# Down projection of a gated MLP in seven half-size products: where two operand sums are formed, who orders VectorE, how far ahead loads are issued, and how the last bank is stored

## The chip, the cores and the metric

The kernel runs on one core of one Trainium2 chip, in one launch that computes one decoder layer. The metric is the device time of the launch in microseconds (us): before the change 1162.03 us, the median of three runs (1159.37, 1162.03 and 1162.38 us).

## What is computed

The layer has three mixing branches (attention, convolution, pooling), an output projection, and a gated MLP. Only the MLP's last step, and the end of the step before it, are touched by the change:

```python
h2 = rms_norm(x, norm2_g[l])
up = h2 @ w_up[l].astype(h2.dtype)                 # 1024 x 5632
up = causal_depthwise_conv(up, ffn_dw_w[l])        # three taps
gate, val = jnp.split(up, 2, axis=-1)
x = x + (jax.nn.silu(gate) * val) @ w_down[l].astype(up.dtype)   # (1024 x 2816) @ (2816 x 1024)
```

All tensors are float32. Call A = silu(gate) * val (1024 tokens x 2816 features), B = w_down, C = A B.

## The kernel before

**Three matmuls for one product.** The matmuls take operands of type fp32r, and each float32 operand is split into two of them: ScalarE casts the high part (`dh`, line 48), VectorE subtracts it from the operand to get the low part (`dl`, line 49). `mm3` (lines 51 to 55) then issues three matmuls, high x high (line 53), high x low (54) and low x high (55). `split` is one such pair of a cast and a subtraction.

**The up projection** runs over 22 feature tiles f, `up(f)` (line 773). Its tail for each f: the last products `prod(..., "3")` and `"22"`; VectorE adds their banks into the tile `u` (line 803 for the value half `uv`, 805 for the gate half `ug`); the three taps are done by ScalarE (768) and twice by VectorE (770); the product `"4"` reuses the bank `b1` that line 803 has read; ScalarE copies it out (812); GpSimd multiplies gate and value (814) and writes the tile to DRAM as `gd[f]` (815). The buffers of pool `ep` (4 buffers) hold `u`, `ws`, `wsh`, `wsl` during this stage; pool `wx` (1 buffer) holds the raw weights `wur`.

**The down projection** starts at line 822. A and B are cut into quadrants (tokens or columns into two halves of 512, features into two halves of 11 tiles of 128), and C is formed from seven quadrant products instead of eight, with sums of quadrants as operands. The work runs in four passes over the 11 feature tiles n, with two sets of four PSUM banks, X and Y (one bank for each 128 tokens x 512 columns):

| pass | steps | operands in X | operands in Y | after the pass, VectorE adds |
|---|---|---|---|---|
| a | 11 | A11, B11 | A12, B21 | X and Y to `acc11`, stored |
| b | 11 | S2 = A22+A21-A11, T2 = B22-B12+B11 | S1 = A21+A22, T1 = B12-B11 | X to `acc12`, Y to `acc22` |
| c | 11 | A11-A21, B22-B12 | A12-S2, B22 | X to `acc22`, stored; Y to `acc12`, stored |
| d | 6 (two tiles n a step, the last one) | A22, B21-T2 | none | X to `acc21`, stored |

The banks go on accumulating from pass to pass. A step is 24 matmuls of 128 x 128 by 128 x 512 (12 for each set of banks, and 12 in the last step of pass d): 38 x 24 + 12 = 924 matmuls. `step_mm` (866) writes one set's 12; `prep(p, n)` (902) forms the sums of step (p, n) on VectorE and splits them; `load(p, n)` (883) issues its DMAs on the queue of SyncE (SP) into a buffer `dr`; `ga` and `wb` (828, 832) load a 128 x 512 piece of A (from `gd`) or of B, 256 KB each.

Before the change `prep` of pass b forms all four sums S1, T1, S2, T2, for which A11 and B11 are loaded again; pass c forms A11-A21. Operands kept from pass to pass (`st`, `ab`, `a11`, the trace's `res`) are loaded a few per step by `load_res`. The buffers `dr` go in turn to `wx`, `ep`, `ep` (`raw_home`, 925), and the sums that are loaded from x (`acc12`, `acc22`) lie in two buffers of `ep`.

**What sets the order.** On SP the order is the program's (`manual_schedule`, 928): loads of step i + 2, then kept operands, in each round of the loop. On VectorE, ScalarE and TensorE a scheduler at build time orders the instructions by readiness and priority; the bank additions `add_to` (857) are given high priority. Stores of finished sums (`store`, 862) are DMAs issued by GpSimd (POOL).

## Time and profile before

| what | us |
|---|---|
| median of three runs | 1162.03 |
| the profiled execution, its own time | 1161.21 |
| its span in the trace | 1159.4 |
| VectorE busy, whole span | 882.5 |
| ScalarE busy, whole span | 576.0 |
| GpSimd busy, whole span | 361.4 |

The profile covers one execution. Its page gives busy times by engine, a chain of work followed back from the end, and groups of instructions by line; the trace can be asked for an engine's instructions in order of time, who waited for whom, and what each engine did in a stretch of the span. In a row of the timeline stand the start, the duration, engine, line, operation, written tile <- read tiles, shape, and in brackets the idle time before it and what ended it. The down projection's first matmul starts at 928.6 us and its last at 1151.9 us.

### The profile page before, as it was taken

The numbers are of one execution on the slowest core, as the hardware profiler recorded it, in microseconds if no ns is written. First come the engines' busy times: TensorE is split into PE (matmuls) and PEld (weight loads), VectorE is DVE, ScalarE is ACT, GpSimd is POOL, SyncE is SP. The second block draws the span as 40 slices with busy tenths as digits, with TensorE's granted clock in tenths as the row PEclk, the third lists the DMA queues.
The fourth block names the chain that finished last, engine by engine and source line by source line (L and its number), as shares of the span: only waits on it lengthen the run. The fifth ranks groups of instructions, "written<-read, shape, count | busy, mean of one in ns | idle before, by whom it ended". The sixth has DMA issues, their size and how long they took to land.

```text
span 1159.4 us, 15556 instructions
## 1 busy us (share of the span) xinstructions
PE 1104.9 (95%) x5684; PEld 921.4 (79%) x5684; DVE 882.5 (76%) x1259; ACT 576.0 (50%) x1045; POOL 361.4 (31%) x373
## 2 busy tenths in 40 slices
PE   7999889999999999879999999999999999899996
PEld 6789889978778878758888888888888788688875
DVE  5798974758998756778877888787878755998673
ACT  8322456688998644445443535353535343233331
POOL 1365597867666653101212121212121210000010
PEclk9999999999999999969999999999999999899999
DMA  9220110022111141211222121312221397672372
GB/s 359 72 81 25 40 28 20 15 74 74 55 48 46 47 154 73 109 37 55 89 75 96 68 96 68 105 59 85 79 98 67 117 328 267 240 263 91 128 235 74
DMA packets 51885, 119.99 MB, mean 103 GB/s; under 512 B 6368, under 2 KB 11872, under 8 KB 48992
## 3 DMA queue, kind: packets, MB, share of 16 engines
q1 hardware_dynamic: 46208, 99.06, 25.8%
q0 software_dynamic: 5600, 19.93, 4.3%
q8 instruction: 45, 0.74, 0.3%
q14 instruction: 32, 0.26, 0.1%
HBM read 94.84 MB, written 19.92 MB: 99 GB/s over the span
## 4 chain that ended last, share of the span: by engine, by line
PE 69%; DVE 10%; issue 7%; DMA 5%; ACT 4%; POOL 3%; SPq 1%; POOLq 0%; ACTq 0%; DVEq 0%
PE b L53 12%; PE b L55 12%; PE b L54 12%; PE mm L53 3%; PE mm L55 3%; PE mm L54 3%; DVE dl L49 3%; PE s L499 2%; DVE acc L257 2%; PE t L523 2%; DMA dr<-in_w_down_dram 2%; PE c L53 1%; PE c L55 1%; PE c L54 1%; DMA dr<-gd 1%
## 5 line engine op out<-in xcount | busy, mean ns | idle before, releaser
L814 POOL TENSOR_TENSOR ac<-ac 128x1024 f32<-128x1024 f32 x22 | 61.5, 2793 | 367.9 <-ACT u L795 207.3
L770 DVE SCALAR_TENSOR_TENSOR ac<-u,par,ac 128x1023 f32<-128x1023 f32 x88 | 112.7, 1280 | 9.6 <-ACT ac L768 8.7
L53 PE MATMUL mm<-w,hh 128*128 128x256 f32 (+1 forms) x384 | 110.3, 288 | 8.5 <-DVE qk L445 4.6
L54 PE MATMUL mm<-w,hh 128*128 128x256 f32 (+1 forms) x384 | 109.5, 285 | 0.6 <-POOL w L49 0.6
L55 PE MATMUL mm<-w,hl 128*128 128x256 f32 (+1 forms) x384 | 109.1, 284 | 0.0
L48 ACT CAST wsh<-ws 128x2048 fp32r<-128x2048 f32 x22 | 42.0, 1910 | 123.5 <-PE b L54 123.3
L257 DVE SCALAR_TENSOR_TENSOR acc<-u,par,acc 128x512 f32<-128x512 f32 x120 | 93.3, 835 | 0.0
L49 DVE TENSOR_TENSOR dl<-dr,dh 128x1024 fp32r<-128x1024 f32 (+1 forms) x39 | 65.6, 1684 | 28.0 <-ACT dh L48 24.9
L511 POOL TENSOR_TENSOR p<-p,l 128x896 f32<-128x896 f32 (+3 forms) x64 | 72.6, 1151 | 44.0 <-DVE l L510 37.5
L48 ACT CAST dh<-dr 128x1024 fp32r<-128x1024 f32 (+1 forms) x39 | 54.7, 1401 | 58.4 <-PE y L55 24.7
L53 PEld LDWEIGHTS mm<-w,hh 128*128 128x128 f32 x384 | 73.0, 190 | 10.1 <-DVE fgt L433 4.8
L49 POOL TENSOR_TENSOR w<-wr,w 128x256 fp32r<-128x256 f32 (+1 forms) x56 | 63.9, 1166 | 42.6 <-ACT w L48 42.3
L54 PEld LDWEIGHTS mm<-w,hh 128*128 128x128 f32 x384 | 73.1, 190 | 1.2 <-POOL w L49 0.8
L55 PEld LDWEIGHTS mm<-w,hl 128*128 128x128 f32 x384 | 73.2, 191 | 0.3
L864 POOL DMA_DIRECT2D out_dram<-acc x16 | 8.7, 542 | 206.9 <-DVE acc L860 206.3
L54 PE MATMUL x<-dl,dh 128*128 128x512 f32 x176 | 69.6, 395 | 3.4 <-DVE dl L49 3.4
L55 PE MATMUL x<-dh,dl 128*128 128x512 f32 x176 | 69.3, 394 | 0.0
L768 ACT ACTIVATE ac<-u,par 128x1024 f32<-128x1024 f32 x44 | 50.7, 1152 | 36.3 <-DVE u L805 35.8
L48 ACT CAST dh<-res 128x1024 fp32r<-128x1024 f32 x22 | 23.1, 1051 | 84.2 <-PE y L55 55.7
L49 DVE TENSOR_TENSOR wsl<-ws,wsh 128x2048 fp32r<-128x2048 f32 x22 | 50.4, 2290 | 12.4 <-ACT wsh L48 12.4
L677 DVE TENSOR_TENSOR ws<-wur 128x512 f32<-128x512 f32 x22 | 59.1, 2688 | 0.0
L53 PE MATMUL x<-dh 128*128 128x512 f32 x176 | 54.0, 402 | 5.2 <-DVE acc L860 4.5
(308 smaller groups left out, 3395.1 us busy)
## 6 DMA issues: line engine op xcount, KB each, us to landing
wur<-in_w_up_dram SPq DMA_DIRECT2D x22, 1024.0 KB, 4.9
dr<-in_w_down_dram SPq DMA_DIRECT2D x66, 256.0 KB, 5.1
dr<-gd SPq DMA_DIRECT2D x55, 256.0 KB, 4.3
gd<-ac POOLq DMA_DIRECT2D x22, 512.0 KB, 3.0
res<-gd SPq DMA_DIRECT2D x22, 256.0 KB, 5.6
wr<-in_w_in_dram SPq DMA_DIRECT2D x40, 128.0 KB, 2.1
v<-in_x_dram SPq DMA_DIRECT2D x8, 512.0 KB, 8.4
wor<-in_w_out_dram SPq DMA_DIRECT2D x16, 256.0 KB, 3.0
```

What stands on the lines that cost most here:

```text
L48: nc.scalar.copy(out=dst_hi, in_=src)
L49: (lo or nc.vector).tensor_tensor(out=dst_lo, in0=src, in1=dst_hi.bitcast(F32), op=ALU.subtract)
L53: nc.tensor.matmul(ps, a_hi, b_hi, start=first, stop=False, skip_group_check=more)
L54: nc.tensor.matmul(ps, a_hi, b_lo, start=False, stop=False, skip_group_check=more)
L55: nc.tensor.matmul(ps, a_lo, b_hi, start=False, stop=last, skip_group_check=more)
L257: nc.vector.scalar_tensor_tensor(out=a, in0=u[:, c, o + j:o + j + 512], scalar=pc(PC_DW + c * CW + j), in1=a, op0=ALU.mult, op1=ALU.add)
L499: nc.tensor.matmul(ps[:, 0:c1 - c0], qT[:, i * P:(i + 1) * P], part[:, c0:c1], start=b == 0, stop=b == 1 and c1 < n)
L511: nc.gpsimd.tensor_tensor(out=pt[:, 0:n], in0=pt[:, 0:n], in1=l[:, 1:2].broadcast_to([P, n]), op=ALU.mult)
L677: nc.vector.tensor_tensor(out=out, in0=a, in1=b, op=ALU.subtract)
L768: nc.scalar.activation(out=ac, in_=us, func=AF.Copy, scale=pc(w0 + 2))
L770: nc.vector.scalar_tensor_tensor(out=ac[:, j:S], in0=us[:, 0:S - j], scalar=pc(w0 + 2 - j), in1=ac[:, j:S], op0=ALU.mult, op1=ALU.add)
L814: nc.gpsimd.tensor_tensor(out=a[:, 1], in0=a[:, 1], in1=a[:, 0], op=ALU.mult)
```

## The change

It has five parts.

1. **Two sums move to pass a.** A11-A21 (in `ab`) and T1 (in `st`) are formed in pass a, where A11 and B11 are in the step's buffer anyway; `a11` becomes `a21`, a copy of A21 kept for pass b. Pass b no longer loads B11, and A11 is not loaded a second time. Per n the number of VectorE sums stays 8: before 4 in pass b, 3 in c, 1 in d; now 2 in a, 3 in b, 2 in c, 1 in d. In pass b the split of the second half of the operands becomes two splits of 128 x 512.
2. **VectorE's order is the program's** in the down projection (`manual_schedule` for DVE): each round splits the next step, forms sums of a step two or three rounds ahead, and adds finished banks at written places. In passes a and b the Y banks' matmuls are written ahead of the X banks'. In the last `up`, `issue_after` puts the gate's taps behind the addition of line 803.
3. **Loads are issued four steps ahead** instead of two, all `dr` buffers are the four of `ep`; `acc22` moves to `wx`, `acc12` to pool `mxa`.
4. **The last two steps** of pass d are written bank by bank, each bank's addition right behind it.
5. **The last store** goes out on SP's queue instead of GpSimd's, and that of the last bank in two halves of 256 columns. `acc12` is added and stored in the first step of pass d.

```diff
         prod(b1, sums, 2, "3", False, True)
-        nc.vector.tensor_tensor(out=uv[:, h1], in0=uv[:, h1], in1=b1, op=ALU.add)
+        added = nc.vector.tensor_tensor(out=uv[:, h1], in0=uv[:, h1], in1=b1, op=ALU.add)
...
-        taps3(a[:, 0], ug, 0, f)
+        with tc.issue_after(added.ins) if f + 1 == NF else ExitStack():
+            taps3(a[:, 0], ug, 0, f)
...
-    homes = iter([(s8, "s8")] * 6 + [(hp2, "hx")] * 8 + [(mxa, "mx")] * 2 + [(ep, "ep")] * 2)
+    homes = iter([(s8, "s8")] * 6 + [(hp2, "hx")] * 8 + [(mxa, "mx")])
...
     def add_to(acc, banks):
         for t in range(4):
-            with tc.high_priority():
-                nc.vector.tensor_tensor(out=acc[:, t], in0=acc[:, t], in1=banks[t], op=ALU.add)
+            nc.vector.tensor_tensor(out=acc[:, t], in0=acc[:, t], in1=banks[t], op=ALU.add)
...
     def load(p, n):
-        r = raw_t[p, n] = slot(*raw_home[len(raw_t) % 3], "dr")
+        r = raw_t[p, n] = slot(ep, "ep", "dr")
...
-        elif p == "b":
-            ga(r[:, 0], "22", n)
-            wb(r[:, 1], "11", n)
-            wb(r[:, 2], "22", n)
...
+        elif p in "bc":
+            ga(r[:, 0], "22" if p == "b" else "12", n)
+            wb(r[:, 1], "22", n)
...
+    def sums(p, n):
         r = raw_t[p, n]
-        if p == "b":
-            nc.vector.tensor_tensor(out=r[:, 0], in0=r[:, 0], in1=ab[n][:, 0], op=ALU.add)
-            sub(r[:, 1], ab[n][:, 1], r[:, 1])
-            sub(st[n][:, 0], r[:, 0], a11[n][:, 0])
-            sub(st[n][:, 1], r[:, 2], r[:, 1])
+        if p == "a":
+            sub(ab[n][:, 0], r[:, 0], a21[n][:, 0])
+            sub(st[n][:, 1], ab[n][:, 1], r[:, 1])
+        elif p == "b":
+            sub(st[n][:, 0], r[:, 0], ab[n][:, 0])
+            nc.vector.tensor_tensor(out=r[:, 0], in0=r[:, 0], in1=a21[n][:, 0], op=ALU.add)
...
+        elif p == "b":
+            part(3, 1, st[n][:, 1:2])
+            part(2, 1, r[:, 0:1])
+            sub(st[n][:, 1], r[:, 1], st[n][:, 1])
+            for s_ in between:
+                sums(*s_)
+            yield
+            part(0, 2, st[n])
...
-    AHEAD, ready = 2, None
-    order = ctx.enter_context(tc.manual_schedule(engines={mybir.EngineType.SP}))
+    AHEAD, N = 4, len(steps)
+    sums_in = {i: [steps[i]] for i in range(NH)}
+    for j in range(NH, N):
+        sums_in.setdefault(j - 3 if j < NH + 2 else j - 2, []).append(steps[j])
+    ctx.enter_context(tc.manual_schedule(engines={mybir.EngineType.SP}))
...
+    ctx.enter_context(tc.manual_schedule(engines={mybir.EngineType.DVE}))
+    for i, (p, n) in enumerate(steps):
+        load_res(2)
+        if i + AHEAD < N:
             load(*steps[i + AHEAD])
...
+            h2 = hl_t[steps[i + 1]]
+            for t in (0, 1):
+                bank_mm(X, h, 2, t, False, False)
+                bank_mm(X, h, 0, t, False, False)
+            for t in range(4):
+                if t > 1:
+                    bank_mm(X, h, 2, t, False, False)
+                    bank_mm(X, h, 0, t, False, False)
+                bank_mm(X, h2, 0, t, False, True)
+                for cs in (slice(0, 256), slice(256, 512)) if t == 3 else (halves[0],):
+                    nc.vector.tensor_tensor(out=acc21[:, t, cs], in0=acc21[:, t, cs], in1=X[t][:, cs], op=ALU.add)
+                    nc.sync.dma_start(out=out[(4 + t) * P:(5 + t) * P, cs], in_=acc21[:, t, cs])
```

How the built program's instructions move is seen at three places.

**The first loads, on SP's queue.** These are the eight DMAs of steps (a, 0) and (a, 1), before:

```order
L830 DMA dr<-gd 128x512 [waits DMASW0_49,DMAHW5_49,DVE_49,Activation_49]
L834 DMA dr<-in_w_down_dram 128x512
L830 DMA dr<-gd 128x512 [waits DMASW3_49]
L834 DMA dr<-in_w_down_dram 128x512
L830 DMA dr<-gd 128x512 [waits DVE_49,PE_49,DMASW1_49,Activation_49,Pool_49]
L834 DMA dr<-in_w_down_dram 128x512
L830 DMA dr<-gd 128x512 [waits DMASW4_49]
L834 DMA dr<-in_w_down_dram 128x512
```

and the same eight after:

```order
L831 DMA dr<-gd 128x512 [waits DVE_49,PE_49,DMASW0_49,Activation_49,Pool_49]
L835 DMA dr<-in_w_down_dram 128x512
L831 DMA dr<-gd 128x512 [waits DMASW3_49]
L835 DMA dr<-in_w_down_dram 128x512
L831 DMA dr<-gd 128x512 [waits DMASW1_49,PE_49]
L835 DMA dr<-in_w_down_dram 128x512
L831 DMA dr<-gd 128x512 [waits DMASW4_49]
L835 DMA dr<-in_w_down_dram 128x512
```

The first step's buffer was that of `wx`; now it is the first one that comes free in `ep`, and its first DMA carries the wait for five engines that the second step's first DMA had.

**The last feature tiles and the first steps, on ScalarE and VectorE.** First ScalarE. `u_8337` and `b1_8334` belong to f = 20, `u_8457` to f = 21; `dh_...<-dr_...` 128x2048 are the casts of steps (a, 0) and (a, 1). Before:

```order
L781 COPY u_8457<-b1_8454 128x512
L48 CAST dh_8584<-dr_8574 128x2048
L812 COPY u_8337<-b1_8334 128x512
L810 ACTIVATE ac_8431<-ac_8431 128x1024
L768 ACTIVATE ac_8431<-u_8337,par_68 128x1024
L797 COPY u_8457<-b3_8456 128x512
L795 COPY u_8457<-b1_8454 128x512
L768 ACTIVATE ac_8536<-u_8457,par_68 128x1024
L810 ACTIVATE ac_8536<-ac_8536 128x1024
L48 CAST dh_8609<-dr_8579 128x2048
```

After:

```order
L781 COPY u_8457<-b1_8454 128x512
L813 COPY u_8337<-b1_8334 128x512
L768 ACTIVATE ac_8431<-u_8337,par_68 128x1024
L811 ACTIVATE ac_8431<-ac_8431 128x1024
L797 COPY u_8457<-b3_8456 128x512
L795 COPY u_8457<-b1_8454 128x512
L768 ACTIVATE ac_8536<-u_8457,par_68 128x1024
L48 CAST dh_8614<-dr_8590 128x2048
L813 COPY u_8457<-b1_8454 128x512
L48 CAST dh_8627<-dr_8595 128x2048
```

The first step's cast stood ahead of the copy of f = 20's last bank (line 812, now 813) and of the scaling behind it (768); it now stands behind them and behind all of f = 21 but one copy.

VectorE at the same place: `u_8457` is the last tile `u`; `ac_8536` its taps; `dl_...<-dr_...` the low parts of steps (a, 0), (a, 1) and on. Before:

```order
L49 TENSOR_TENSOR dl_8585<-dr_8574,dh_8584 128x2048
L770 SCALAR_TENSOR_TENSOR ac_8431<-u_8337,par_68,ac_8431 128x1023
L770 SCALAR_TENSOR_TENSOR ac_8431<-u_8337,par_68,ac_8431 128x1022
L805 TENSOR_TENSOR u_8457<-u_8457,b3_8456 128x512
L770 SCALAR_TENSOR_TENSOR ac_8536<-u_8457,par_68,ac_8536 128x1023
L803 TENSOR_TENSOR u_8457<-u_8457,b1_8454 128x512
L770 SCALAR_TENSOR_TENSOR ac_8536<-u_8457,par_68,ac_8536 128x1022
L49 TENSOR_TENSOR dl_8610<-dr_8579,dh_8609 128x2048
```

After:

```order
L770 SCALAR_TENSOR_TENSOR ac_8431<-u_8337,par_68,ac_8431 128x1023
L770 SCALAR_TENSOR_TENSOR ac_8431<-u_8337,par_68,ac_8431 128x1022
L805 TENSOR_TENSOR u_8457<-u_8457,b3_8456 128x512
L803 TENSOR_TENSOR u_8457<-u_8457,b1_8454 128x512
L770 SCALAR_TENSOR_TENSOR ac_8536<-u_8457,par_68,ac_8536 128x1023
L49 TENSOR_TENSOR dl_8615<-dr_8590,dh_8614 128x2048
L770 SCALAR_TENSOR_TENSOR ac_8536<-u_8457,par_68,ac_8536 128x1022
L49 TENSOR_TENSOR dl_8628<-dr_8595,dh_8627 128x2048
```

The addition of line 803 now stands ahead of both taps of the last gate, and the low part of the first step, which stood ahead of all of these, stands behind it.

**VectorE at the change from pass a to pass b.** `x0` to `x3` and `y0` to `y3` are the banks, line 860 (now 856) their addition to `acc11`. Before:

```order
L677 TENSOR_TENSOR res_8595<-res_8600,res_8595 128x512
L905 TENSOR_TENSOR dr_9043<-dr_9043,res_8595 128x512
L860 TENSOR_TENSOR acc_8855<-acc_8855,x1_8565 128x512
L677 TENSOR_TENSOR res_8589<-dr_9003 128x512
L860 TENSOR_TENSOR acc_8855<-acc_8855,x2_8566 128x512
L677 TENSOR_TENSOR dr_9043<-res_8595,dr_9043 128x512
L860 TENSOR_TENSOR acc_8855<-acc_8855,x3_8567 128x512
L860 TENSOR_TENSOR acc_8855<-acc_8855,y0_8568 128x512
L49 TENSOR_TENSOR dl_9014<-res_8588,dh_9013 128x1024
L49 TENSOR_TENSOR dl_9014<-dr_8952,dh_9013 128x1024
```

After:

```order
L677 TENSOR_TENSOR res_8580<-res_8586,dr_8844 128x512
L856 TENSOR_TENSOR acc_8574<-acc_8574,y0_8568 128x512
L856 TENSOR_TENSOR acc_8574<-acc_8574,y1_8569 128x512
L856 TENSOR_TENSOR acc_8574<-acc_8574,y2_8570 128x512
L856 TENSOR_TENSOR acc_8574<-acc_8574,y3_8571 128x512
L49 TENSOR_TENSOR dl_8994<-res_8575,dh_8993 128x1024
L856 TENSOR_TENSOR acc_8574<-acc_8574,x0_8564 128x512
L856 TENSOR_TENSOR acc_8574<-acc_8574,x1_8565 128x512
L856 TENSOR_TENSOR acc_8574<-acc_8574,x2_8566 128x512
L856 TENSOR_TENSOR acc_8574<-acc_8574,x3_8567 128x512
L49 TENSOR_TENSOR dl_9044<-res_8575,dh_9043 128x512
L49 TENSOR_TENSOR dl_9044<-dr_8920,dh_9043 128x512
```

The bank additions, which were mixed with the sums of coming steps, now stand in two runs of four, Y ahead of X, with the split of one operand between them.

On TensorE the last 12 matmuls of the program stand in the same order as before (first the four high x high, then the two others of bank x0, of x1, of x2, of x3). In pass a each step's eight high x high matmuls stand ahead of its sixteen others, Y's banks ahead of X's; at the first step of pass b the order is y0, y1, y2, y3, x0, x1, x2, x3 with all three matmuls of a bank together, and a few high x high matmuls of the step behind it in between.

More of the change, by code (lines that the diff above doesn't have):

```diff
@@ L909, in prep, with halve, part @@
         elif p == "c":
             sub(r[:, 0], r[:, 0], st[n][:, 0])
-            sub(ab[n][:, 0], a11[n][:, 0], ab[n][:, 0])
             sub(ab[n][:, 1], r[:, 1], ab[n][:, 1])
-        elif p == "d":
+        else:
             for j in range(min(2, NH - n)):
                 sub(r[:, 2 * j + 1], r[:, 2 * j + 1], st[n + j][:, 1])
-        h = hilo()
+    def halve(p, n, between=()):
+        r = raw_t[p, n]
+        h = hl_t[p, n] = hilo()
+        def part(i, q, src):
+            split(h[0][:, i:i + q], h[1][:, i:i + q], src)
@@ new lines, in tile_hybrid_block @@
+    AHEAD, N = 4, len(steps)
[3 more added lines that the diff above has]
+    ctx.enter_context(tc.manual_schedule(engines={mybir.EngineType.SP}))
+    acc11 = slot(mxa, "mx", "acc")
+    st += packed(2, NH, homes)
+    ab += packed(2, NH, homes)
+    a21 += packed(4, NH, homes)
+    for m in range(NH):
+        res_q += [(ga, a21[m][:, 0], "21", m), (wb, ab[m][:, 1], "12", m)]
+    for i in range(AHEAD):
+        load(*steps[i])
+        if i == AHEAD - 2:
+            load_res(4)
@@ new lines, in tile_hybrid_block @@
+    for _ in halve(*steps[0]):
+        pass
+    ctx.enter_context(tc.manual_schedule(engines={mybir.EngineType.DVE}))
+    for i, (p, n) in enumerate(steps):
+        load_res(2)
+        if i + AHEAD < N:
+            load(*steps[i + AHEAD])
+        if (p, n) == ("a", NH - 4):
+            load_acc(acc11, 0, 0)
+        if (p, n) == ("b", NH - 4):
+            acc12 = load_acc(slot(mxa, "mx", "acc"), 0, 1)
+            acc22 = load_acc(slot(wx, "wx", "acc"), 1, 1)
+        if (p, n) == ("c", NH - 4):
+            acc21 = load_acc(slot(mxa, "mx", "acc"), 1, 0)
+        now = sums_in.pop(i, [])
+        inside = i + 1 < N and steps[i + 1][0] == "b"
+        part_2 = halve(*steps[i + 1], now) if i + 1 < N else iter(())
+        if p == "a" and not inside:
+            next(part_2, None)
+        if not inside:
+            for s_ in now:
+                sums(*s_)
+        last = i + 1 == N or steps[i + 1][0] != p
+        next(part_2, None)
+        if not (last and inside):
+            next(part_2, None)
+        if (p, n) == ("d", 0):
+            add_to(acc12, Y)
+            store(acc12, 0, 1)
+        h = hl_t[p, n]
+        if p == "d" and i + 2 == N:
+            h2 = hl_t[steps[i + 1]]
[10 more added lines that the diff above has]
+                    nc.sync.dma_start(out=out[(4 + t) * P:(5 + t) * P, cs], in_=acc21[:, t, cs])
+            break
+        if p == "d":
+            step_mm(X, h, 2, False, False)
+            step_mm(X, h, 0, False, False)
+            continue
+        for banks, at in ((X, 0), (Y, 2)) if p == "c" or (p, n) == ("b", NH - 1) else ((Y, 2), (X, 0)):
+            step_mm(banks, h, at, n == 0 and (p == "a" or p == "b" and banks is Y), last)
+            if not last or p == "c" and banks is Y:
+                continue
+            if p == "a":
+                add_to(acc11, banks)
+                next(part_2, None)
+            else:
+                add_to(acc12 if p == "b" and banks is X else acc22, banks)
+        if last and p == "a":
+            store(acc11, 0, 0)
+        if last and p == "c":
+            store(acc22, 1, 1)
```

70 lines of the change are left out of this document (10 added, 60 removed).

## The prediction

> **What bounds the kernel now.** I read the page first: its head, the engines' shares, the clock and the chain.
>
> ```profile
> span 1159.4 us, 15556 instructions
> ...
> PE 1104.9 (95%) x5684; PEld 921.4 (79%) x5684; DVE 882.5 (76%) x1259; ACT 576.0 (50%) x1045; POOL 361.4 (31%) x373
> ...
> PEclk9999999999999999969999999999999999899999
> ```
>
> TensorE (PE) is busy for 95% of the span, so a gain can only come from where it stands still, or from the tail. Next I asked who waited for whom on PE from 924 us on, which is the stretch that the change touches (columns: total us, times, longest):
>
> ```profile
> PE x L53 <- DVE acc L860: 4.5, 4, 1.9
> PE x L54 <- DVE dl L49: 3.4, 3, 2.3
> PE b L53 <- DVE u L803: 1.2, 1, 1.2
> PE x L53 <- ACT dh L48: 0.5, 1, 0.5
> PE x L53 <- ACT u L812: 0.2, 1, 0.2
> ```
>
> Ten waits, 9.8 us. They understate the loss, as the timeline of PE shows:
>
> ```profile
> 924.15 0.40 PE L55 MATMUL b<-t3h,wsl 128*128 128x512 f32 x1
> 925.75 0.50 PE L53 MATMUL b<-t4h,wuh 128*128 128x512 f32 x1 [1.20 <-DVE u L803]
> ...
> 940.90 0.39 PE L53 MATMUL y<-dh 128*128 128x512 f32 x1
> ...
> 946.34 0.39 PE L53 MATMUL y<-dh 128*128 128x512 f32 x1
> ...
> 988.72 0.39 PE L55 MATMUL y<-dh,dl 128*128 128x512 f32 x1
> 991.02 0.47 PE L53 MATMUL x<-dh 128*128 128x512 f32 x1 [1.91 <-DVE acc L860]
> ...
> 1151.92 0.39 PE L55 MATMUL x<-dh,dl 128*128 128x512 f32 x1
> ```
>
> A step of 24 matmuls takes 946.34 - 940.90 = 5.44 us, 0.227 us a matmul from start to start, though one lasts 0.39. Over the wait at 991 the starts are 2.30 apart, 2.07 more than the pace, where the row says 1.91 idle; the next start comes about 0.1 late too. So a wait costs its idle time and 0.27. From 924.15 to 1151.92 are 227.8 us with 12 + 924 starts, worth 936 x 0.2267 = 212.2: **15.6 us are lost**. Waits and restarts explain 9.8 + 2.7 = 12.5. Most of the rest is here (the columns are the stretch, busy times, granted clock, DMA share, GB/s):
>
> ```profile
> 930.00:990.00 60.00, 58.90 (x259) 48.14 (x257) 35.74 (x26) 22.15 (x15) 2.98 (x2) 1.00 0.86 303
> ...
> 991.80:998.60 6.80, 5.87 (x14) 4.13 (x13) 6.80 (x11) 0.00 (x0) 0.54 (x1) 0.50 0.11 41
> ```
>
> Right after the wait at 991 the granted clock is 0.50 for 6.8 us, and a matmul takes 0.43: some 11 of them lose 0.2 each, 2.3 us. Then there is the tail, from PE's last start to the end of the span 7.5 us:
>
> ```profile
> L864 POOL DMA_DIRECT2D out_dram<-acc x4: 539/539/542, 1152.0 to 1153.8; - x4
> DMA to landing us min/median/max: 2.3/2.7/3.0
> ...
> L1033 POOLq DRAIN  x3: 40/93/4927, 1153.7 to 1159.2; - x3
> L1033 SPq DRAIN  x3: 7/7/7, 1157.2 to 1158.9; - x3
> ```
>
> The last store, issued at 1153.8, has landed by 1156.8, and SP is through at 1157.2; but GpSimd's drain behind its stores lasts from 1153.7 for 4.93 us, to 1158.7, and the program ends 0.7 later.
>
> **The change part by part.** All sums are made against the profiled execution's own 1161.2 us (span 1159.4), 0.8 below the median of the runs. Ahead of 913 us nothing is moved.
>
> *The start of pass a.* These rows are of ScalarE, VectorE and SP, in the last two feature tiles:
>
> ```profile
> 913.26 1.91 ACT L48 CAST dh<-dr 128x2048 fp32r<-128x2048 f32 x1 [0.75 <-PE b L54]
> 915.07 0.58 ACT L812 COPY u<-b 128x512 f32<-128x512 f32 x1
> ...
> 916.51 1.14 ACT L768 ACTIVATE ac<-u,par 128x1024 f32<-128x1024 f32 x1
> 915.20 2.29 DVE L49 TENSOR_TENSOR dl<-dr,dh 128x2048 fp32r<-128x2048 f32 x1 [0.67 <-ACT dh L48]
> 917.68 1.28 DVE L770 SCALAR_TENSOR_TENSOR ac<-u,par,ac 128x1023 f32<-128x1023 f32 x1 [0.19 <-ACT ac L768]
> 925.01 0.68 DVE L803 TENSOR_TENSOR u<-u,b 128x512 f32<-128x512 f32 x1
> 904.63 0.33 SPq L830 DMA_DIRECT2D dr<-gd  x1
> 920.44 0.33 SPq L830 DMA_DIRECT2D dr<-gd  x1
> 921.75 0.43 SPq L834 DMA_DIRECT2D dr<-in_w_down_dram  x1
> DMA to landing us min/median/max: 2.6/4.1/4.8
> SPq L830 <- DVE ac L770: 13.8, 1, 13.8
> ```
>
> Line 803's bank ends at 924.55 (924.15 + 0.40), so the addition can start at 924.65 and not 925.01: **-0.4**. X's last bank now comes last in its step and no longer waits for line 812's copy: 0.2 + 0.27, **-0.45**.
>
> Against that, the first step loses its early load. Before, its data came at 904.63 into `wx`, and cast and low part were made at 913 to 917.5. In the new order its first DMA has the wait that the second step's had, and that one went out at 920.44, after 13.8 us of waiting for f = 20's last two taps (917.68, two of 1.28). These taps now come earlier, since the cast of 1.91 no longer stands ahead of the copy and the scaling that they need: the copy starts at 913.5 (the wait of the first row ends for it too), the scaling follows at 914.1 to 915.2, the taps end at 917.9. The four DMAs then go out from 918.0 to 919.4 and have landed 4.8 later, by 924.2; the cast ends at 926.1. VectorE has line 803 to 925.3 and one tap (1.2) ahead of the low part: 926.5 to 928.8. PE comes out of the up projection at 928.2 (925.4 and 12 matmuls), does one high x high matmul and wants the low part at 928.45: a **new wait of 0.4**, with its restart 0.7.
>
> A second one is close behind: the fourth load waits for f = 21's last tap, which stands behind the low parts of steps 0 and 1 and two sums, at about 937.9. It lands 4.9 later, cast and low part end at 947.1, and PE wants them at 946.7: 0.5 more. Together **+1.2**. The bounds are 0 (taps and loads as early as ScalarE allows) and 3.5 (loads stay at 920.4: low part at 930.9, a wait of 2.5, and 1.0 at the fourth).
>
> *From pass a to pass b.* The loss before is 1.91 + 0.93 of line 860's waits, 0.5 + 0.2 of the ones behind them, four restarts (1.1) and 2.3 of half clock: 6.9 us. The rows for the new order:
>
> ```profile
> L677 DVE TENSOR_TENSOR res<-dr,res 128x512 f32<-128x512 f32 x9 | 6.2, 684 | 0.2 <-DMA dr<-in_w_down_dram 0.2
> L49 DVE TENSOR_TENSOR dl<-res,dh 128x1024 fp32r<-128x1024 f32 x9 | 10.9, 1216 | 0.0
> 1056.96 1.28 DVE L860 TENSOR_TENSOR acc<-acc,x 128x512 f32<-128x512 f32 x2
> ```
>
> Two additions in 1.28 of which one takes 0.68: they follow each other by 0.6; a 1024-wide low part takes 1.2. Let T be the start of step (a, 10). VectorE, from the cast at T - 3.3, does 2.29 and four sums to T + 1.4, two 512-wide splits and three sums to T + 4.4, Y's additions to T + 6.9, a split to T + 8.1, X's additions from T + 8.7 to T + 10.5. PE, at 0.227 a matmul in the new order, asks for y0 at T + 5.4 (ready 5.0), y3 at 8.2 (6.9), x0 at 9.1 (8.7), x3 at 11.1 (10.5). Each is met, by 0.4 to 1.3. In step (b, 1) ScalarE's cast for (b, 2), which must wait for PE to leave (b, 0), stands ahead of a cast that PE needs: 0.2. So 6.7 of 6.9 go: **-6.7**. What hides the additions is 0.4 us of slack; with that gone, half might stay (3.4).
>
> The VectorE work itself is the same 8 sums; two of them lie in pass a, where before it idles most of a step (35.7 of 60 us busy), and pass b falls to 3 x 0.6 + 2.4 of 5.44.
>
> *Later changes of pass.* From b to c, c to d and in d the waits are 0.45 + 1.19 (the rest of line 860's 4.5), and 0.87 + 2.28 (line 49), with four restarts 5.9. The first two go, as X's additions now run while Y's 12 matmuls do. The last two are late loads:
>
> ```profile
> 1135.04 0.69 DVE L677 TENSOR_TENSOR dr<-dr,res 128x512 f32<-128x512 f32 x1 [2.88 <-DMA dr<-in_w_down_dram]
> ...
> SPq L830 <- DMA out_dram<-acc: 8.2, 2, 7.6
> ```
>
> SP waited 8.2 us for stores to leave buffers that `dr` shared with the sums. `dr` now shares with none, and is asked for four steps (20 us) ahead: **-5.8**. The range is -3.5 to -5.9.
>
> *The tail.* TensorE's last 12 matmuls keep their order, so writing them bank by bank changes nothing there. Two half additions cost between 0.68 and 1.36 together; I take 0.7. Stores on SP are issued as each addition ends, the last at about 1153.6, and land in 2.6 (the least of the loads above) to 3.0: about 1156.4. GpSimd's drain will have begun 30 us earlier, behind `acc12`'s stores; if it then is over, SP's end at 1156.9 and 0.7 give 1157.6 to 1157.9: **-1.5**, between 0 (five stores queue up, as the loads' 4.8 allows) and -2.0.
>
> The Trainium skill, "DMA: Bandwidth & Descriptors", section "Latency and other measured facts", puts the first byte at about 0.6 us on SP's path and 1 us on GpSimd's; by that the tail would gain 0.4 more. The rows have 2.3 for GpSimd's quickest store and 2.6 for SP's quickest load, so I give it nothing.
>
> Sum: -0.4 - 0.45 + 1.2 - 6.7 - 5.8 - 1.5 = -13.65, which gives 1147.5 on the profiled execution's scale. The runs' median lies 0.8 above it; between the two I put the **forecast at 1148 us**.
>
> **The rivals.**
>
> *The first loads stay late, and the wait trips the clock.* With loads at 920.4 PE waits 2.5 us near 929, 2.3 more than forecast with the fourth load's: 1150.3. Waits of such a length have been followed by the half clock, or not:
>
> ```profile
> 1139.30 0.50 PE L54 MATMUL x<-dl,dh 128*128 128x512 f32 x1 [2.28 <-DVE dl L49]
> ```
>
> 1.91 at 991 was followed by 6.8 us of it, 2.28 here was not. A stretch of 3.4 (half of that seen) costs 1.7, one of 6.8 costs 3.4: up to 1153.7. For it: the wait for five engines in the order. Against: ScalarE's new order frees the buffer 2.4 us sooner.
>
> The Trainium skill, "TensorE: Matmul & The Clock Gate", section "Part 1: The HAM clock gate (the "warmup" mystery)", has the clock halve after at least one idle window of some 3.4 us, of a counter that runs free. By that rule no wait here trips it and this rival ends at 1150.3; the trace disagrees, since a wait of 1.91 us was enough.
>
> *The written order blocks VectorE.* A low part or a sum that waits holds up all behind it, where a scheduler let others pass. With its 0.4 us of slack gone at the change to pass b, half or all of the 6.7 stays: 1151.4 to 1154.7. Against: the schedule above, from rows.
>
> *Slower: the loads of pass a.* A step of pass a now moves six pieces of 256 KB (5.5 before), and a load goes out only when sums have freed its buffer. In 5.44 us that needs 289 GB/s. From there on it decides: at 213 GB/s a step takes 7.4, and nine steps (two of eleven are loaded ahead) lose 17, which brings 1148 to 1165, 0.3% above before. Against: 303 GB/s on the average of 930 to 990, with the DMA engines at 0.86.
>
> *The change does not do what it says:* stores on SP bring nothing (1.5), and the late cast of (b, 2) comes back in each step of pass b, as ScalarE's order is still the scheduler's, 10 x 0.2: 1151.5.
>
> **How the numbers follow.** Forecast 0.58; late loads 0.20; VectorE blocked 0.11; the last rival 0.06; slower 0.03; 0.02 for a change too small to be told. The predicted time is the likeliest case's. The range starts at the forecast with the start's wait gone (1.2), the tail's best (0.5) and the runs' own spread (they span 3 us; 1.5 of it): 1144.8. Upward it takes in the late loads with the shorter stretch of half clock (1152.0) and half of the blocked case with the tail's 1.5 (1152.9): 1153.5. Outside lie some 0.15. About 0.3% (3.5 us) is what a measurement of this kernel can tell from no change; faster by more than that, below 1158.5, are all cases but the last two: 0.94; the same 0.03, slower 0.03.
>
> **What would show it.** PE's waits from 924 us on: L803 at about 0.8; one of about 0.4 for `dl` L49 near 928.5; one of some 0.3 near 947; none for `acc` beyond 0.3; none for `dl` in pass d. SP's first `dr` load at about 918, and no wait for `out_dram`. Granted clock 1.00 through the change to pass b. The last matmul near 1140, the span ending 6 us behind it, GpSimd's long drain away from the end. I am wrong if the first loads stand at 920.4 or later, if `acc` is waited for by 1 us or more, or if PE waits for `dl` at each step of pass a with the DMA share near 1.0.

## The result, and the profile after

The changed kernel takes 1144.49 us (median of four runs, 1144.37 to 1147.07) where the kernel before takes 1162.2 (four runs, 1159.37 to 1162.59): a ratio of 0.9858, with a 95% interval of 0.9837 to 0.9879. It is faster by 17.7 us, or 1.4%. The forecast was 1148 us; the median lies 0.3 us below the lower end of the range (1144.8), and the profiled execution, at 1147.07 the longest of the four, inside it.

The head of its page, for the same places as before:

```profile
span 1145.3 us, 15552 instructions
...
PE 1101.0 (96%) x5684; PEld 919.9 (80%) x5684; DVE 882.5 (77%) x1271; ACT 578.1 (50%) x1056; POOL 363.3 (32%) x369
...
PEclk9999999999999999969999999999999999999999
```

VectorE is as busy as before, to a tenth; its work has only moved. The slice of lower clock near 1000 us (the 8) is gone; the one near 500 us (the 6), ahead of the change, stays. Who waited for whom on PE from 915 us on (total us, times, longest):

```profile
PE y L53 <- ACT dh L48: 1.1, 1, 1.1
PE b L53 <- DVE u L803: 0.8, 1, 0.8
PE y L54 <- DVE dl L49: 0.3, 2, 0.2
```

Four waits and 2.2 us are left of ten and 9.8. No `acc` and no `dl` in pass d is among them. The timeline of PE has them all ahead of 950 us, at the start of pass a:

```profile
925.19 0.50 PE L53 MATMUL b<-t4h,wuh 128*128 128x512 f32 x1 [0.78 <-DVE u L803]
...
928.59 0.50 PE L54 MATMUL y<-dl,dh 128*128 128x512 f32 x1 [0.15 <-DVE dl L49]
...
946.39 0.50 PE L53 MATMUL y<-dh 128*128 128x512 f32 x1 [1.05 <-ACT dh L48]
...
948.72 0.50 PE L54 MATMUL y<-dl,dh 128*128 128x512 f32 x1 [0.19 <-DVE dl L49]
...
1140.39 0.39 PE L55 MATMUL x<-dh,dl 128*128 128x512 f32 x1
```

From the last of them to the last matmul PE keeps its pace of 0.227 us. At the change to pass b the stretch of the former waits reads like this, first before, then after (us of the stretch, busy times of PE, PE's loads, VectorE, ScalarE and GpSimd, granted clock, DMA share, GB/s):

```profile
988.00:1010.00 22.00, 18.46 (x66) 13.45 (x66) 20.14 (x31) 5.88 (x6) 2.17 (x4) 0.84 0.62 218
```

```profile
930.00:990.00 60.00, 58.73 (x257) 47.57 (x256) 43.16 (x42) 23.19 (x15) 6.11 (x2) 1.00 0.87 304
988.00:1010.00 22.00, 22.00 (x97) 17.72 (x96) 21.27 (x32) 8.64 (x12) 2.17 (x4) 1.00 0.49 172
```

PE is busy for all of 22 us where it was for 18.46, at a clock of 1.00. In pass a VectorE now has 43.2 of 60 us (35.7 before), and the loads still run at 304 GB/s: the sixth piece of a step does not slow them.

The tail is 4.9 us from the last matmul to the end of the span, where it was 7.5. Its rows (the stores, and the engines' drains at the program's end):

```profile
L993 SPq DMA_DIRECT2D out_dram<-acc x5: 333/338/422, 1140.2 to 1142.3; - x5
...
DMA to landing us min/median/max: 2.0/2.2/2.2
```

```profile
L1069 POOLq DRAIN  x3: 40/102/6474, 1118.2 to 1145.0; - x3
L1069 SPq DRAIN  x3: 7/7/7, 1144.5 to 1144.8; - x3
```

GpSimd's long drain begins at 1118.2, behind `acc12`'s stores, and is over at 1124.7, 20 us ahead of the end. The last store goes out at 1142.3 and lands 2.0 later, at 1144.3; SP's drain comes at 1144.5 and the span ends at 1145.3.

### The profile page after: what moved, and what is told of

It reads as the page before. It is cut to its first block, busy times and chain, and to the rows that moved or that the text cites. A ratio compares the mean times of both kernels' runs of the same rounds, so it can differ in the third digit from the quotient of the medians.

```text
span 1145.3 us, 15552 instructions
## 1 busy us (share of the span) xinstructions
PE 1101.0 (96%) x5684; PEld 919.9 (80%) x5684; DVE 882.5 (77%) x1271; ACT 578.1 (50%) x1056; POOL 363.3 (32%) x369
## 5 line engine op out<-in xcount | busy, mean ns | idle before, releaser
L815 POOL TENSOR_TENSOR ac<-ac 128x1024 f32<-128x1024 f32 x22 | 64.6, 2934 | 372.0 <-ACT u L795 190.4
L511 POOL TENSOR_TENSOR p<-p,l 128x896 f32<-128x896 f32 (+3 forms) x64 | 72.5, 1148 | 44.1 <-DVE l L510 37.6
L49 DVE TENSOR_TENSOR dl<-dr,dh 128x2048 fp32r<-128x2048 f32 (+2 forms) x39 | 58.8, 1509 | 25.6 <-ACT dh L48 25.6
L48 ACT CAST dh<-dr 128x2048 fp32r<-128x2048 f32 (+2 forms) x39 | 49.9, 1279 | 53.4 <-PE x L55 16.4
L48 ACT CAST dh<-res 128x1024 fp32r<-128x1024 f32 (+1 forms) x33 | 29.8, 908 | 74.5 <-issue 27.8
L49 DVE TENSOR_TENSOR pt<-t,pt 128x512 fp32r<-128x512 f32 (+1 forms) x80 | 49.9, 631 | 9.0 <-ACT pt L48 8.7
```

The costliest lines, as they stand in the source:

```text
L48: nc.scalar.copy(out=dst_hi, in_=src)
L49: (lo or nc.vector).tensor_tensor(out=dst_lo, in0=src, in1=dst_hi.bitcast(F32), op=ALU.subtract)
L511: nc.gpsimd.tensor_tensor(out=pt[:, 0:n], in0=pt[:, 0:n], in1=l[:, 1:2].broadcast_to([P, n]), op=ALU.mult)
L815: nc.gpsimd.tensor_tensor(out=a[:, 1], in0=a[:, 1], in1=a[:, 0], op=ALU.mult)
```

## Experiments

Profiles are compared in one way: over all of PE's matmuls from 915 us on, each start that comes over 0.15 us later than the pace of 0.227 is counted with what it comes late, its restart in it. "L803" is the wait for line 803's addition. "Start" is pass a up to 950 us (before the change its 0.38 is X's last bank). The next two columns are the changes of pass, with pass d in the second. "Tail" goes from the start of the last matmul to the end of the span.

| kernel | median us (runs) | 4600 at | L803 | start | a to b | b to c, c to d, d | tail |
|---|---|---|---|---|---|---|---|
| before | 1162.2 (4) | 890.3 | 1.37 | 0.38 | 6.99 | 5.43 | 7.5 |
| changed, first profile | 1144.49 (4) | 890.2 | 0.95 | 2.07 | 0 | 0 | 4.9 |
| e1 changed, again | 1144.57 (5) | 888.6 | 0.95 | 0.70 | 0 | 0 | 4.9 |
| e2 last stores on GpSimd | 1147.66 (4) | 888.0 | 0.95 | 2.82 | 0 | 0 | 7.6 |
| e3 last bank whole | 1146.22 (4) | 890.1 | 0.95 | 1.72 | 0 | 0 | 4.9 |
| e4 no edge for the taps | 1145.02 (4) | 888.7 | 1.37 | 1.04 | 0 | 0 | 4.9 |
| e5 T1 in pass b | 1145.80 (4) | 889.2 | 0.95 | 1.74 | 0.66 | 0 | 5.2 |
| e6 Y's additions later | 1146.04 (4) | 890.1 | 0.95 | 1.94 | 0.99 | 0 | 4.9 |
| e7 VectorE's order free | 1155.54 (8) | 889.8 | 0.95 | 2.02 | 0.82 | 9.67 | 4.9 |
| e8 three steps ahead | 1145.74 (4) | 890.2 | 0.95 | 0.76 | 0.92 | 0 | 4.9 |
| e9 X ahead of Y | 1146.42 (4) | 888.3 | 0.95 | 1.55 | 1.65 | 0 | 4.9 |
| e10 one sum in the loads' slots | 1145.12 (4) | 890.2 | 0.95 | 3.06 | 0 | 0.16 | 4.9 |
| e11 start of pass a mended | 1142.75 (4) | 890.0 | 0 | 0 | 0 | 0 | 4.9 |
| e12 two sums in the loads' slots | 1171.47 (4) | 889.4 | 0.95 | 2.21 | 0 | 25.97 | 4.9 |

The columns from "4600 at" on are of the one profiled execution, which is not the median one; "4600 at" is where PE's matmul number 4600 (counted from 0) starts, ahead of everything that the change touches. Executions differ there by up to 2.3 us, so an edit is judged by its own column and the median only bears it out.

**e1, the changed kernel again.** No edit.

> The changed kernel once more, nothing edited. Its profiled execution took 1147.07 us, its three others 1144.4. Theory (the changed stretch has one schedule): a second profile shows the same stretch, PE's loss from 924 us to its last matmul 4.6 us within 0.6 and the end 4.9 us behind the last matmul; if this execution is one of 1144.4, the 2.7 us are gone ahead of 924 us. Rival (the loads at the start of pass a land differently from execution to execution): the 2.7 us are in the waits for dh and dl between 928 and 949, 2.1 us in the first profile.

```profile
PE b L53 <- DVE u L803: 0.8, 1, 0.8
PE y L54 <- DVE dl L49: 0.4, 2, 0.2
```

These are PE's waits from 915 us on: the one of 1.1 for `dh` is not there. This execution took 1143.78 us, 3.3 less than the first profile's. Of these, 1.4 are at the start of pass a (2.07 against 0.70), and 1.6 lie ahead of the change: matmul 4600 starts at 888.58 and not at 890.17. So each theory had about half. The start of pass a depends on when loads land. The second load's last piece landed 4.6 us after its issue here and 5.7 in the first profile, and the fourth load, which waits for work behind the second, went out 1.05 us earlier against matmul 4600. Over the seven profiles whose edit leaves the start as it is (the first one, e1 to e3, e6, e10 and e12) the last piece of the fourth load lands 52.4 to 55.1 us behind matmul 4600, and the start costs 0.7 to 3.1, in the same order but for one pair 0.1 apart.

**e2 and e3, the tail.** In e2 the last stores are GpSimd's again, in e3 the last bank is one piece:

```diff
-                    nc.sync.dma_start(out=out[(4 + t) * P:(5 + t) * P, cs], in_=acc21[:, t, cs])
+                    nc.gpsimd.dma_start(out=out[(4 + t) * P:(5 + t) * P, cs], in_=acc21[:, t, cs])
```

```diff
-                for cs in (slice(0, 256), slice(256, 512)) if t == 3 else (halves[0],):
+                for cs in (halves[0],):
```

> The five last stores issued by GpSimd again, the additions still bank by bank and the last in two halves. Theory (the end is GpSimd's drain, which ends 1.9 us behind the last landing, against about 0.2 on SP, and GpSimd's stores land in 2.3 to 3.0 where SP's took 2.0 to 2.2): 2.0 to 2.9 us slower than e1, all of it behind the last matmul, which keeps its place within 0.3. Rival (the prediction's sizing, the drain is worth 1.5): 1.2 to 1.7 slower. Second rival (issue is the price: five issues of 0.6 on GpSimd): over 3 slower.

> The last bank added and stored whole (128x512) on SP, not in two halves. Theory (the halves save nothing that the end waits for): the last addition starts at the same time, takes 0.68 where the two halves took 0.75 together, its store is issued 0.1 earlier and lands 0.1 to 0.2 later; within 0.3 of e1. Rival (half a bank's transfer is what the end waits for): 0.4 to 0.8 slower.

The stores and drains of e2:

```profile
L993 POOL DMA_DIRECT2D out_dram<-acc x5: 539/539/542, 1138.7 to 1141.0; - x5
...
DMA to landing us min/median/max: 2.3/2.6/2.9
```

```profile
L1069 POOLq DRAIN  x3: 40/93/4610, 1141.0 to 1146.1; - x3
```

The last store is issued at 1141.0, 2.3 behind the last matmul (1138.7), and lands 2.6 later. The drain begins at 1141.0 and lasts 4.61, to 1145.6, 2.0 behind that landing. The tail is 7.64 us, 2.7 more than e1's, as the theory of the drain had it (2.0 to 2.9) and the prediction's 1.5 had not; the medians differ by 3.1. Of the 2.7, the later issue makes 0.4 (2.3 against 1.9 behind the last matmul) and the landing 0.6 (2.6 against 2.0); the rest is the way from the last landing to the end, 2.73 against 0.96. In e3 the tail is 4.87: the halves of the last bank save nothing. Its median is 1.7 above e1's, but its profile has 1.0 more at the start and matmul 4600 1.5 later (890.05), and nothing at the place of the edit.

**e4, the taps' edge.**

```diff
-        with tc.issue_after(added.ins) if f + 1 == NF else ExitStack():
+        with ExitStack():
```

> The edge that puts the last gate taps behind line 803's addition is taken out. Theory (the prediction's -0.4): the tap of 1.28 goes ahead of line 803 again, PE's wait for it is 1.2 in place of 0.8, and the kernel is 0.3 to 0.5 slower at that point; the taps end earlier, so the fourth load goes out up to 1.2 earlier and gives 0.5 to 1.2 of the wait at 946 back: between 0.7 faster and 0.5 slower in all. Rival (the order's gain is a gain in the whole): 0.4 slower.

```profile
PE b L53 <- DVE u L803: 1.2, 1, 1.2
```

PE's wait at line 803 is that of before again, 0.42 more than e1's with its restart: the size of the prediction's term. The fourth load's first DMA goes out 12.1 us behind the matmul that waits for line 803 (936.21 against 924.15), in e1 11.8: the taps that end earlier bring it nothing.

**e5 and e6, the change to pass b.** In e5 T1 is formed in pass b from B11, which is loaded again. In e6 the additions of Y stand behind a low part:

```diff
             sub(ab[n][:, 0], r[:, 0], a21[n][:, 0])
-            sub(st[n][:, 1], ab[n][:, 1], r[:, 1])
         elif p == "b":
+            sub(st[n][:, 1], ab[n][:, 1], r[:, 2])
             sub(st[n][:, 0], r[:, 0], ab[n][:, 0])
```

```diff
-                add_to(acc11, banks)
-                next(part_2, None)
+                if banks is X:
+                    next(part_2, None)
+                    add_to(acc11, Y)
+                    add_to(acc11, X)
```

> One of the two sums goes back: T1 = B12 - B11 is formed in pass b from a reloaded B11 (11 loads of 256 KB and 11 subtractions leave pass a for pass b). Theory (the change to pass b was mended by where the additions stand; in its three steps one subtraction of 0.6 goes and one comes): PE's waits at the change to pass b stay under 0.5, in pass b VectorE has 4.8 of a step's 5.44 and no wait over 0.3 comes, the kernel is within 0.6 of e1, or faster by up to 1 where pass a's loads land earlier. Rival (the sum formed early is what makes the room, its slack was 0.3 to 0.6): the additions come 0.6 to 1.8 later, waits for acc of 0.6 to 3 return, 0.9 to 3.5 slower.

> The additions of Y at the end of pass a stand behind the low part of (b, 0)'s second half (1.2 us) in VectorE's order; those of X stay. Theory (the additions had 0.3 us of slack): PE waits 0.9 for y0, then less for each next bank since additions follow at 0.6 and PE asks every 0.7, none for x0; 0.9 to 1.3 slower, no half clock. Rival (the place of the additions is not what counts, the room is made by sums formed early): under 0.4.

B11 is still loaded in pass a for its own product, so the 11 loads do not leave pass a, where the expectation has them leave it; pass b has 11 more. In e5 two late starts of 0.24 and 0.42 come at the change to pass b, and nothing later: undoing the early T1 costs 0.7 of the 7 us there. (Its tail of 5.2 stays unexplained; nothing there was edited.) For e6, the timelines of VectorE, ScalarE and PE:

```profile
989.36 1.22 DVE L49 TENSOR_TENSOR dl<-res,dh 128x1024 fp32r<-128x1024 f32 x1
990.49 2.47 DVE L856 TENSOR_TENSOR acc<-acc,y 128x512 f32<-128x512 f32 x4
```

```profile
990.59 0.62 ACT L48 CAST dh<-res 128x512 fp32r<-128x512 f32 x1 [1.27 <-PE x L55]
```

```profile
991.32 0.47 PE L53 MATMUL y<-dh 128*128 128x512 f32 x1 [0.82 <-ACT dh L48]
```

The first addition ends at 991.17 (990.49 and 0.68) and PE starts on y0 at 991.32, 0.99 late. The row names the cast, which ends last, at 991.21; but in e1 the same cast ends at 988.26, when PE has been on y0 since 987.39. So it is the addition, and an order of 1.2 us the other way costs 0.99: the slack of about 0.3 was all there was.

**e7, VectorE's order.** Sums, loads and bank order stay; the scheduler orders VectorE.

```diff
-    ctx.enter_context(tc.manual_schedule(engines={mybir.EngineType.DVE}))
...
-            nc.vector.tensor_tensor(out=acc[:, t], in0=acc[:, t], in1=banks[t], op=ALU.add)
+            with tc.high_priority():
+                nc.vector.tensor_tensor(out=acc[:, t], in0=acc[:, t], in1=banks[t], op=ALU.add)
```

> VectorE's order is the scheduler's again (the line that writes it down is out, the additions have their priority back); loads, sums and bank order stay as changed. In its order one sum stands between y0 and y1, and a low part of 1.2 and one of 0.6 with a sum between x0 and x1. Theory (the written order is a small part of the gain): waits for acc of 0.3 to 1.5 at the change to pass b, 0.3 to 2.0 slower. Rival (the written order carries the gain): 3.4 to 6.9 slower with the half clock back. Null: within 0.3 of e1.

PE's waits from 1000 us on, and VectorE's timeline ahead of the longer one (line 857 is the additions' here):

```profile
PE x L53 <- DVE acc L857: 3.5, 1, 3.5
PE y L53 <- DVE acc L857: 1.8, 1, 1.8
```

```profile
1116.41 0.69 DVE L677 TENSOR_TENSOR dr<-dr,res 128x512 f32<-128x512 f32 x1 [3.22 <-DMA dr<-in_w_down_dram]
1117.02 2.28 DVE L49 TENSOR_TENSOR dl<-dr,dh 128x2048 fp32r<-128x2048 f32 x1
1119.23 1.28 DVE L857 TENSOR_TENSOR acc<-acc,x 128x512 f32<-128x512 f32 x2
```

It is 11 us slower than e1, 9.7 of it at the changes from b to c and c to d, and only 0.8 at the change to b. The scheduler put a sum of a later step ahead of X's additions; the sum's load was not there, VectorE stood for 3.22 us, and the additions behind it, whose banks had long been done, came at 1119.2. PE waited 3.5, and half clock followed each of the two waits (the windows of the first one are shown below). None of the three cases expected had this: the theory of a small part was right at the change to b, and the size is beyond the rival's, at two other places.

**e8, three steps ahead.**

```diff
-    AHEAD, N = 4, len(steps)
+    AHEAD, N = 3, len(steps)
...
-        if i == AHEAD - 2:
+        if i == 2:
```

> Loads three steps ahead, not four; the slots of the loads are still shared with no sum. Theory (what cost before was the sharing of slots with the sums; three steps are 16 us and a load lands in 4 to 6.5): no wait for dl in passes c and d over 0.4; but the sums of (b, 0) and (b, 1) now ask for data that is issued in the same step, so VectorE waits 4 to 6 us in each of two steps and the additions behind come late: 1 to 5 slower, all of it at the change to pass b. Rival (distance was the price): waits for dh or dl of 0.8 and more in c and d as well. Null: within 0.5.

```profile
980.30 0.69 DVE L677 TENSOR_TENSOR res<-dr,res 128x512 f32<-128x512 f32 x1 [1.69 <-DMA dr<-gd]
...
989.38 2.47 DVE L856 TENSOR_TENSOR acc<-acc,y 128x512 f32<-128x512 f32 x4
```

VectorE waits 1.69 us for (b, 0)'s load, once and not twice for 4 to 6; the additions come too late for y0, and PE starts 0.92 late. In passes c and d there is no wait: three steps are far enough there, and the fourth is needed only where the early sums ask for pass b's data.

**e9, X ahead of Y.**

```diff
-        for banks, at in ((X, 0), (Y, 2)) if p == "c" or (p, n) == ("b", NH - 1) else ((Y, 2), (X, 0)):
+        for banks, at in ((X, 0), (Y, 2)):
...
-                next(part_2, None)
+                if banks is X:
+                    next(part_2, None)
```

> X's banks stand ahead of Y's in passes a and b again (products and additions), and the low part of (b, 0)'s second half behind X's additions; the written order, the early sums and the loads stay. Theory (what mends the change to pass b is that Y, whose operands are ready first, goes first): PE takes x0 to x3 in time and then asks for the low part, made at 989 to 990.2 in e1's times, and for y0, added at 990.8, both wanted at 988.3: waits of 1.7 to 2.5 in all there, 2.0 to 2.8 slower with restarts, 1.6 to 3.4 more if over 1.9 of one stretch of 3.4 stand idle (half clock). At the start of pass a X's last bank asks early again: up to 0.47 more. Rival (the additions between the two products are enough, either way round): under 0.6.

```profile
PE x L54 <- DVE dl L49: 1.6, 3, 0.7
```

Of the three waits for a low part one of 0.6 is at the change to b, 0.91 late with its restart and behind two short ones for X's additions, 0.37 each: 1.65. The one of 0.7 is at the start of pass a, 0.88 late where e1 has 0.33. The bank order is the largest single part that was undone there, a little under what the theory had (2.0 to 2.8), and the half clock did not come.

**e10 and e12, the slots of the loads.** In e10 `acc22` takes one of the four slots, in e12 `acc12` as well:

```diff
-            acc12 = load_acc(slot(mxa, "mx", "acc"), 0, 1)
-            acc22 = load_acc(slot(wx, "wx", "acc"), 1, 1)
+            acc12 = load_acc(slot(ep, "ep", "acc"), 0, 1)
+            acc22 = load_acc(slot(ep, "ep", "acc"), 1, 1)
```

> acc22 takes one of the four slots of the loads, from the end of pass b to its stores at the end of pass c; nothing else. Theory (a load that asks for a slot held by a sum waits for its stores, as before): SP waits for out_dram at the change from c to d, PE waits for dl or dh in pass d, 2 to 5 us in all. Rival (three slots are enough, loads go round the held one): no wait for out_dram on SP, PE's waits in c and d within 0.4 in all, the kernel within 0.5 of e1. Second rival (three slots delay every load from the end of b on): waits of 0.5 to 1 in each step of c, over 5 slower.

> Both acc12 and acc22 in slots of the loads, as before the change, so that two of the four slots are left for the loads of c and d; VectorE's written order and every other line stay. Theory (it was the two slots left that made the loads of pass d late, whatever number of steps ahead they are asked for; one slot taken was covered in e10): SP waits over 5 us for out_dram, a load goes out when the low part two steps ahead is made, PE waits for dl or dh in passes c and d by 2 to 5 us in all, 2.0 to 5.5 slower than e10 outside the start of pass a. VectorE's sums of a step stand two steps ahead in its written order, so a late load holds up the low part behind it and the wait may be longer than the 3.4 of before. Rival (the written order and early sums alone removed the waits of pass d, slots count for nothing): PE's waits in c and d within 0.5.

SP's wait for stores in e10, and then in e12 PE's waits from 1000 us on and SP's:

```profile
SPq L831 <- DMA out_dram<-acc: 2.8, 1, 2.8
```

```profile
PE x L54 <- DVE dl L49: 13.5, 10, 3.5
PE x L53 <- DVE acc L856: 4.0, 1, 4.0
```

```profile
SPq L831 <- DMA out_dram<-acc: 7.7, 2, 7.1
```

With one sum in the slots SP does wait for its stores, but PE loses 0.16: the load has 20 us of lead to spend. With two, a load goes out only two steps ahead, SP waits 7.7 us, nearly the 8.2 of before, and the kernel is 27 us slower than the changed one and slower than before (ratio 1.0099, 1.0081 to 1.0117). Pass c alone now loses 0.75 to 1.3 in each step from 1068 us on, which before it did not. VectorE's waits, from 1040 us on:

```profile
DVE dr L677 <- DMA dr<-gd: 24.0, 9, 3.3
DVE dr L677 <- DMA dr<-in_w_down_dram: 19.5, 8, 3.9
```

In the written order a sum stands two steps ahead of its use, and a load that is late by that measure stops VectorE for 2.6 us each time, with the low parts that PE needs next behind it.

**e11, towards a faster kernel.** The first load goes into `wx` again, and the last feature tile's products are taken in the order 2, 1, 3, 22, 4 (by the same kind of edge as the taps', on TensorE: `m2` and `m3` are the last matmuls of the products "2" and "3", and `behind` puts what it holds after them):

```diff
-        r = raw_t[p, n] = slot(ep, "ep", "dr")
+        r = raw_t[p, n] = slot(*((wx, "wx") if (p, n) == ("a", 0) else (ep, "ep")), "dr")
...
-        prod(b3, sums, 0, "1", True, True)
+        with behind(m2):
+            prod(b3, sums, 0, "1", True, True)
...
-        prod(b3, sums, 3, "22", False, True)
+        with behind(m3):
+            prod(b3, sums, 3, "22", False, True)
```

> Towards a faster kernel: the first step's load goes into wx, as before the change, so that each later load of pass a takes a slot one step earlier; and in the last feature tile TensorE's products are taken in the order 2, 1, 3, 22, 4, so that 12 matmuls (2.7 us) stand between product 3 and product 4, which waits for line 803's addition of 0.7. Theory: the wait for line 803 (0.95 with its restart) goes, the low part of the first step is ready (0.3), the fourth load no longer hangs behind f = 21's last tap (0 to 2.1 by execution): 1.2 to 3.4 faster than e1's kernel, loss from 924 us on under 0.8. Rival (ScalarE's cast at 913 delays the taps and the second load goes out at 920.4 again): a wait of 0.3 to 1.5 at the second step, 0 to 1.2 faster.

SP's first loads, and the stretch from 924 us to the last matmul:

```profile
904.30 0.33 SPq L837 DMA_DIRECT2D dr<-gd  x1
...
920.10 0.33 SPq L837 DMA_DIRECT2D dr<-gd  x1
```

```profile
924.00:1137.00 213.00, 213.00 (x937) 175.11 (x936) 165.06 (x190) 79.51 (x75) 11.39 (x14) 1.00 0.57 194
```

PE is busy for 213.00 of 213 us. The second load does go out at 920.1, as the rival had it, but PE asks for it 5.4 us later than for the first and never waits. The median is 1142.75 us (1141.88 to 1143.56; ratio to before 0.984, 0.9823 to 0.9857), 1.8 below e1's; its slowest run is below the fastest of the changed kernel's nine, 1143.78, though not on the same chip.

## Why the prediction was right, and where it was off

Term by term, between the two profiled executions:

| step | predicted | measured |
|---|---|---|
| line 803 | -0.4 | -0.42 |
| X's last bank | -0.45 | -0.38 |
| start of pass a | +1.2 | +2.07 |
| from a to b | -6.7 | -6.99 |
| b to c, c to d, d | -5.8 | -5.43 |
| tail | -1.5 | -2.6 |
| sum | -13.65 | -13.75 |

The executions differ by 14.1 (1161.21 and 1147.07); 0.1 of the rest lies ahead of the change and 0.25 in scatter of the pace. So the sum was right to 0.5 us, and part of that is luck: the start of pass a and the tail missed by 0.9 and 1.1, in opposite directions. The median moved by 17.7, 3.6 more than the two profiled executions: the changed kernel's is 2.6 above its median, by what e1 shows, and the one before is 1.0 below its own. That is why the forecast of 1148 is 0.9 above the profiled execution and 3.5 above the median.

*Line 803* was right, and e4 shows it. *X's last bank* was right in size; which of the two, the bank order or ScalarE's order, took the wait away was not shown: in e9, with X first again, it did not come back.

*The start of pass a* had the right mechanism and was too small. The first load went out at 917.92 as the prediction had it (918.0) and PE waited 0.31 with its restart for the low part. The fourth load went out at 938.03 (937.9), but the wait behind it was sized at 0.5 and is 1.57 (1.21 and 0.36). The landings are those of its last three pieces:

```profile
938.03 0.33 SPq L831 DMA_DIRECT2D dr<-gd  x1
...
939.36 0.42 SPq L835 DMA_DIRECT2D dr<-in_w_down_dram  x1
...
DMA to landing us min/median/max: 3.3/4.2/4.8
...
944.43 1.90 ACT L48 CAST dh<-dr 128x2048 fp32r<-128x2048 f32 x1 [7.39 <-DMA dr<-in_w_down_dram]
```

The step that was off is "It lands 4.9 later". The last of its four pieces did take 4.8 from its own issue (939.36 to 944.2), but the four go out over 1.3 us, which the prediction counts for the first load (918.0 to 919.4) and leaves out for this one: it landed 6.2 behind the first issue. So the cast ended at 946.3 and not at 944.8. PE was due at the high part at 945.2 (three steps of 5.44 from 928.6 are 944.9) and started 1.21 late, a wait that the prediction did not have. The low part is wanted eight matmuls later, for which the 946.7 was right, and cost 0.36. Other executions have up to 3.1 here, within the bounds of 3.5 on which the prediction let this term run; e11 takes all of it away.

*From a to b* came out in size, and the schedule held to tenths: the additions of Y stand at 986.4 in e1, PE takes y0 at 987.39. What carries it was left open, and the runs tell part of it: undone alone, the bank order costs 1.65, the additions' place 0.99, loads four ahead 0.92, the written order 0.82, the early T1 0.66. No part carries the 7 us; each is good for about one, as the slack is 0.3 and anything later than that shows. Added up they are 5.0 of the 7. The other early sum, and all parts undone together, were not tried, so what makes the rest stays open.

*b to c, c to d and d* came out too, but by a reason that the prediction had as a risk. "The written order blocks VectorE" was a rival of 0.11; e7 shows the opposite, that with sums made two and three steps ahead the scheduler's order is what blocks, for 9.7 us, more than the 5.4 that was lost before. The rival's mechanism is real all the same: e8 and e12 show that a written order passes on every late load. That `dr` "now shares with none, and is asked for four steps ahead" holds as a pair, with room in each: in passes c and d three steps ahead and no sharing will do (e8), and four steps ahead with one slot shared (e10, 0.16 lost); with two slots shared the lead is gone too, and it does not (e12). Two steps ahead with no sharing was not run.

*The tail* is the term that was mis-sized by most, outside its own bounds (0 to -2.0). I took 2.6 to 3.0 for a store's landing, from loads and GpSimd's stores, and 1.2 from there to the end; SP's stores land in 2.0 to 2.2, the last one in 2.0, and the end comes 1.0 behind. The prediction gave nothing for the two paths' landings; between e2 and e1 the last one differs by 0.6. That GpSimd's drain holds the end up, ending 1.9 to 2.0 us behind its last landing, is shown by e2. That writing the last banks in halves costs nothing is shown by e3, and that it brings nothing, too.

In the chances, the four cases of a clear gain add up to 0.95 where the text has 0.94; nothing hangs on it. The rivals: the first loads did not stay at 920.4; pass a did not run short of rate (304 GB/s, and PE busy for 58.73 of 60 us). And the change did what it says: the stores on SP brought their part, and ScalarE's order cost no wait in pass b.

## What to carry to other kernels

Write an engine's order down only together with the lead of its loads: here the order with late loads was slower than before by 1% (e12), and all the rest of the change without the order brought 4.7 us of some 16 (e7, beside runs of before with a median of 1160.25). When sums are moved ahead, ask of each what it waits for and what stands behind it on its engine; a sum that waited 3.2 us for a load ahead of an addition that was ready cost PE 3.5 us and the half clock behind (e7). Ask of the stores that end a program what the end waits for: here one word in a line was worth 2.7 us (e2).
